# Attention scores as 64-row products in the two halves of TensorE's rows, in place of stacked 128-row products

## The chip, the cores and the metric

The kernel runs on one core of a Trainium2 chip. The metric is the device time of one execution in microseconds. Each run gives one time; the median of the runs is compared.

## The reference

One decoder block on x of 2048 positions and 1024 channels, with two branches that share a projection of the normalised input. The first branch is a gated linear recurrence (RG-LRU). The second is differential attention with 8 heads. Each head has two components of 64 channels, with softmax scores of their own, whose difference weighs v:

```python
u = rmsnorm(h, pre_g[l])
z = jnp.einsum('bsd,df->bsf', u, w_in[l])
xr, zr, q, k, v, za, gm = jnp.split(z, split_points, axis=-1)
...
s = jnp.einsum('bqhcd,bkhcd->bhcqk', q[:, q0:q1], k[:, :q1]).astype(jnp.float32) * scale
mask = (q0 + jnp.arange(Q_BLOCK))[:, None] >= jnp.arange(q1)[None, :]
s = jnp.where(mask, s, -jnp.inf)
p = jax.nn.softmax(s, axis=-1)
w = p[:, :, 0] - lam * p[:, :, 1]
outs.append(jnp.einsum('bhqk,bkhe->bqhe', w.astype(v.dtype), v[:, :q1]))
```

The attention's output is normalised and gated, both branches are projected, merged by sigmoid gates, projected once more, normalised and added to x. All inputs are float32.

## The kernel before

**Precision.** [...] To come near float32, an operand is split into a high and a low half of 16 bits (hi + lo), and a product a*b is made of hi*hi, hi*lo and lo*hi, added in PSUM. `mm3` (L187) does this for the projections: 8 blocks of 128 channels, 3 products each, 24 matmuls of 512 columns for one group.

**Stages.** First the recurrent branch (to about 488 us in the trace), then the attention (to about 1957 us), then the branches' projections and the output (to the end).

**The attention.** Its work is cut into units: one head h and one block t of 128 queries, so 8 x 16 units. Unit t has t + 1 blocks of 128 keys. `pieces` (L796) cuts these into one piece of up to 8 blocks (1024 columns) for t < 8, and two pieces from t = 8 on. A unit goes through these steps:

- `a_scores(u, ci)` (L800): the scores of component ci. For each piece it takes a PSUM tile `sc` of 128 x 1024 (the pool has two) and fills it in chunks of up to 512 columns, two matmuls a chunk (L814). VectorE then copies the piece to SBUF and takes its row maximum (L826), with the mask on the last block (L830).
- `a_exp` (L837): the bias from the maxima on VectorE (L845) and the exponentials on ScalarE (L851).
- `a_comb` (L854): VectorE combines the two components (L874), ScalarE rounds to the high half (L876), GpSimd makes the low half (L877), and two transposing DMAs on SP's queue bring both to `pt` (L880).
- `a_pv` (L886): the product with v, three matmuls of 128 columns for each block of keys (L897).

**How hi and lo are stacked.** A component has 64 channels, half of the array's 128 rows. K is kept as a tile of 128 rows for each component: its high half in rows 0 to 63, its low half in rows 64 to 127. Q is kept in two versions, (hi, lo) and (lo, hi). The matmul v = 0 gives hi*hi + lo*lo, the matmul v = 1 gives lo*hi + hi*lo, both over 128 rows. The projection, however, leaves both components side by side in the rows. So `split16` (L665) makes the halves in a tile `st` (ScalarE L667, VectorE L668), and `g_k` and `g_q` (L672, L685) copy pieces of `st` to their places by DMA on SP's queue: 4 transfers for a K tile, 6 for a Q tile. The copies are put into the list `later` and issued behind the next projection group.

**The order of work.** Between the attention's steps stand projection groups: k and q (`g_k`, `g_q`), v with its gate (`g_va`, 96 matmuls of 256 columns), and merge gates (`g_gm`). They are listed in `fills` (L743 to L763), together with entries that prepare weights and carry no group. Before a unit starts, all that it needs is made (`fill_to`, L946); beyond that, an accumulator lets in about (t + 10)/10 entries for each unit (L947, `per` is 28 for a head). The order within a unit is the string `ORD = "0fc1eFp"` (L35, L949): scores of component 0, one projection group if due, combination of the unit before, scores of component 1, exponentials, all other groups that are due, product with v of the unit two before (`LAG`). The framework's scheduler may still move instructions against each other where data allow.

Of the kernel before, what the change touches and what calls it, by code (L numbers as in the profile page):

```python
# [24 lines left out]
CH = 512  # L25
# [3 lines left out]
GM_T = 8   # groups of gate projections kept for the end of the attention  # L29
LAG = 2    # units between a unit's scores and its product with v  # L30
ACC0 = 8.0  # projection groups ahead of the attention units
PD = 5     # x tiles loaded ahead
# order in an attention unit: scores (0, 1), exponentials (e), combination of the unit before (c),
# product with v of an earlier one (p), with projection groups between them (f: one, F: all that are due)
ORD = "0fc1eFp"  # L35
SEG_A = 2  # where a head's gate projections stand between its chunks
# [7 lines left out]
def p2(e):  # L44
    return float(2.0 ** e)
# [3 lines left out]
def kernel(  # L49
# [44 lines left out]
    with ExitStack():  # L94
# [38 lines left out]
        def w16_at(i):  # L133
            """one of the four places for a block of weights"""
            return lambda w: w16_p.tile([128, 2, KD, 128], F16, tag=f"w{i % 4}", name="w16")
# [24 lines left out]
        def w_scale(w, ps, fac, keep=None):  # L160
            """power of two that brings the block's norm close to 2^13 (a rough sum is enough for it)"""
# [25 lines left out]
        def mm3(ps, w, c0, n):  # L187
            """ps[f128, n] += w^T u over all of d, s in [c0, c0 + n)"""
# [7 lines left out]
        # ================= RG-LRU branch =================  # L196
        with ExitStack() as lx:
# [21 lines left out]
            def prep_g(gr):  # L219
                """power of two that keeps the scaled, normalised input in fp16's range"""  # L220
# [58 lines left out]
            # weight pipeline  # L279
# [17 lines left out]
            def in_half(b, hf, z, w):  # L297
                """PSUM tile of a half row of an x_r (z = 0) or z_r (z = 1) block"""
# [144 lines left out]
            # per-channel vectors: rows of 128 channels, turned into columns  # L443
# [25 lines left out]
            with tc.issue_after(x_last[1]):  # L469
                # block-diagonal gate weights, exact f32r hi/lo  # L470
# [14 lines left out]
            with after_x():  # L485
                nc.vector.tensor_scalar(out=ba, in0=ba, scalar1=0.5, scalar2=None, op0=ALU.mult)
                nc.vector.tensor_scalar(out=bx, in0=bx, scalar1=0.5, scalar2=None, op0=ALU.mult)
                # softplus(-a) = max(-a, 0) + log1p(exp(-|a|)), log1p(t) = 2 atanh(t / (2 + t))
# [87 lines left out]
        # ================= differential attention and merge gates =================  # L576
# [3 lines left out]
        with ExitStack() as ax:  # L580
# [33 lines left out]
            def wadv(n):  # L614
                """weight blocks up to index n ready; two more on their way"""
# [49 lines left out]
            def split16(ps):  # L665
                st = sp.tile([128, 2, CH], F16, tag="st", name="st")
                nc.scalar.activation(st[:, 0], ps, AF.Copy, scale=p2(-14))  # L667
                nc.vector.scalar_tensor_tensor(out=st[:, 1], in0=ps, scalar=p2(-14), in1=st[:, 0],  # L668
                                               op0=ALU.mult, op1=ALU.subtract)
                return st  # L670

            def g_k(h, c):  # L672
                ps = ps_m.tile([128, CH], F32, tag="mm", name="mm")
                mm3(ps, wl["k", h], c * CH, CH)
                st = split16(ps)
                t = kp.tile([128, 2, CH], F16, tag="K", name="K")

                def mv():
                    for i in range(2):
                        nc.sync.dma_start(out=t[0:64, i, :], in_=st[64 * i:64 * i + 64, 0, :])  # L680
                        nc.sync.dma_start(out=t[64:128, i, :], in_=st[64 * i:64 * i + 64, 1, :])
                later.append(mv)
                Kt[h, c] = t

            def g_q(h, c):  # L685
                ps = ps_m.tile([128, CH], F32, tag="mm", name="mm")
                mm3(ps, wl["q", h], c * CH, CH)
                st = split16(ps)
                t = qp.tile([128, 2, 2, CH], F16, tag="Q", name="Q")

                def mv():
                    for i in range(2):
                        nc.sync.dma_start(out=t[0:64, :, i, :], in_=st[64 * i:64 * i + 64, :, :])
                        nc.sync.dma_start(out=t[64:128, 0, i, :], in_=st[64 * i:64 * i + 64, 1, :])
                        nc.sync.dma_start(out=t[64:128, 1, i, :], in_=st[64 * i:64 * i + 64, 0, :])
                later.append(mv)
                Qt[h, c] = t
# [102 lines left out]
            def a_scores(u, ci):  # L800
                h, t = u.h, u.t
                if ci == 0:
# [3 lines left out]
                col = 0  # L806
                for pi, (b0, nb) in enumerate(pieces(t)):
                    ps = ps_s.tile([128, 1024], F32, tag="sc", name="sc")
                    for x in range(0, nb, 4):
                        m = min(4, nb - x) * 128  # L810
                        K = Kt[h, (b0 + x) // 4]
                        q0 = (t % 4) * 128
                        for v in range(2):
                            nc.tensor.matmul(ps[:, x * 128:x * 128 + m], Qt[h, t // 4][:, v, ci, q0:q0 + 128],  # L814
                                             K[:, ci, 0:m], start=(v == 0), stop=(v == 1))
# [7 lines left out]
                    last = b0 + nb == t + 1  # L823
                    m = (nb - 1 if last else nb) * 128
# [384 lines left out]
```

## Time and profile before

| | |
|---|---|
| median of 3 runs | 2505.45 us (2501.87 to 2505.91) |
| span of the profiled execution, from its first to its last instruction | 2506.1 us |
| mean granted TensorE clock | 0.980 |
| DMA: packets, bytes | 541323, 268.73 MB |

No time other than the span is recorded for the profiled execution, so the span stands for it. It lies 0.65 us above the median of the runs.

In the profile, PE is TensorE's matmuls and PEld its weight loads, DVE is VectorE, ACT ScalarE, POOL GpSimd, and SP the queue that issues most DMAs. L814 is line 814 of the kernel. A row of a group has the line, the engine, the operation, output <- inputs, the shape and the count; behind the first bar the busy time in us and the mean of one in ns, and behind the second bar the engine's idle time just before, with what ended most of it. A row of waits reads: who waited, for whom, us in total, times, longest. A row of the timeline starts with the start and the length in us. A row of DMAs has the count, the size of one and the us from issue to landing. A row of a stretch has its length, then busy time and count of PE, PEld, DVE, ACT and POOL, the granted clock, the DMA share and GB/s.

### The profile page before, as it was taken

The page shows a single profiled execution, that of the slowest core. Times are in us where ns is not written, and L with a number is a line of the kernel's source. Part 1 is how long each engine was busy: PE and PEld are TensorE (multiplying, and loading weights), DVE is VectorE, ACT ScalarE, POOL GpSimd, SP SyncE. Part 2 cuts the span into 40 slices and gives each one's busy share as a digit, 9 for nine tenths or more (in the row PEclk, how much of TensorE's full clock was granted, in tenths as well). Part 3 has the DMA queues.
Part 4 walks back from the last instruction along what each step waited for, and adds up shares of the span by engine and source line. Part 5 has one row for each costly group of instructions (what it writes and reads, how often), then busy time and mean ns, then how long its engine had stood idle before and what let it go on. Part 6 is the DMA issues. An engine that isn't in the chain of part 4 may idle for free. (4 is left out here: it accounts for less than half of the span.)

```text
span 2506.1 us, 41430 instructions
## 1 busy us (share of the span) xinstructions
PE 2353.1 (94%) x15240; PEld 1355.3 (54%) x15240; DVE 1548.4 (62%) x4316; ACT 1224.6 (49%) x2156; POOL 679.7 (27%) x415
## 2 busy tenths in 40 slices
PE   6789999999998999998998999999999899999998
PEld 5344444465665665665665655655655444444443
DVE  8877667668658566667567478468467244633323
ACT  5555545456547546556456457356456244312211
POOL 3443334212222212222222222223123133322211
PEclk9899999999999999999999999999999999999999
DMA  9511111235444534635535445445445854743202
GB/s 244 104 43 48 46 42 34 76 81 119 108 96 111 113 84 108 127 82 113 115 84 114 103 96 118 95 90 124 95 90 115 251 177 135 239 148 118 84 17 101
DMA packets 541323, 268.73 MB, mean 107 GB/s; under 512 B 370504, under 2 KB 518016, under 8 KB 541120
## 3 DMA queue, kind: packets, MB, share of 16 engines
q1 hardware_dynamic: 538144, 256.74, 42.6%
q0 software_dynamic: 2816, 9.08, 1.2%
q8 instruction: 119, 1.95, 0.3%
q14 instruction: 84, 0.69, 0.1%
q10 hardware_dynamic: 160, 0.27, 0.0%
HBM read 110.79 MB, written 41.94 MB: 61 GB/s over the span
## 5 line engine op out<-in xcount | busy, mean ns | idle before, releaser
L192 PEld LDWEIGHTS <-w 128*128 128x128 f16 x5040 | 475.9, 100 | 576.5 <-issue 89.2
L192 PE MATMUL mm<-uT,w 128*128 128x512 f16 x3072 | 705.1, 383 | 12.9 <-ACT gm L728 8.9
L877 POOL TENSOR_TENSOR e<-e,e 128x1024 f16<-128x1024 f32 (+2 forms) x192 | 317.0, 1666 | 970.6 <-ACT e L876 487.0
L851 ACT ACTIVATE e<-e,nb,sc_h 128x1024 f32<-128x1024 f32 (+7 forms) x384 | 376.1, 980 | 160.8 <-DVE nb L845 125.6
L826 DVE TENSOR_SCALAR_CACHE_REDUCE e<-sc 128x1024 f32<-128x1024 f32 (+7 forms) x352 | 305.2, 880 | 134.9 <-PE sc L814 122.3
L192 PE MATMUL ps<-uT,w 128*128 128x512 f16 (+1 forms) x1968 | 354.4, 345 | 26.1 <-ACT xr L318 17.7
L711 PE MATMUL mm<-wva,uT 128*128 128x256 f16 x3072 | 352.7, 275 | 3.3 <-DVE st L668 2.6
L1094 PE MATMUL psb<-yt,w 128*128 128x512 f16 x1536 | 332.9, 379 | 2.0 <-ACT w L177 1.5
L711 PEld LDWEIGHTS <-uT 128*128 128x128 f16 x3072 | 301.5, 99 | 48.8 <-issue 2.9
L814 PE MATMUL sc<-K,Q 128*128 128x512 f16 (+3 forms) x1280 | 287.2, 351 | 19.9 <-DVE e L826 13.8
L897 PE MATMUL o<-V,pt 128*128 128x128 f16 x3264 | 224.5, 222 | 38.4 <-DMA pt<-e 38.1
L1094 PEld LDWEIGHTS <-w 128*128 128x128 f16 x1536 | 149.1, 98 | 184.9 <-issue 3.9
L897 PEld LDWEIGHTS <-pt 128*128 128x128 f16 x3264 | 200.0, 99 | 72.8 <-DMA pt<-e 46.5
L876 ACT ACTIVATE e<-e 128x1024 f16<-128x1024 f32 (+2 forms) x192 | 150.1, 802 | 143.1 <-DVE e L874 118.5
L814 PEld LDWEIGHTS <-Q 128*128 128x128 f16 x1280 | 119.6, 99 | 133.2 <-issue 20.2
L874 DVE SCALAR_TENSOR_TENSOR e<-e,rs,e 128x1024 f32<-128x1024 f32 (+2 forms) x192 | 190.0, 1017 | 2.2
L1125 PE MATMUL psf<-wo,m 128*128 128x512 f16 x720 | 155.7, 379 | 0.0
L156 ACT ACTIVATE jk<-wst 128x1024 bf16<-128x1024 f32 x80 | 84.2, 1052 | 138.7 <-DMA wst<-in_w_in_dram 102.6
L1125 PEld LDWEIGHTS <-m 128*128 128x128 f16 x768 | 75.1, 98 | 90.6
L1098 DVE SCALAR_TENSOR_TENSOR t<-gt,psb 128x512 f32<-128x512 f32 x64 | 43.8, 686 | 120.2 <-PE psb L1094 100.1
L1148 ACT ACTIVATE jk<-psf 128x1024 bf16<-128x1024 f32 x15 | 15.4, 1024 | 134.0 <-PE psf L1125 69.4
L717 DVE SCALAR_TENSOR_TENSOR V<-mm,V 128x256 f16<-128x256 f32 x64 | 26.9, 421 | 85.7 <-ACT V L716 85.6
(247 smaller groups left out, 2417.3 us busy)
## 6 DMA issues: line engine op xcount, KB each, us to landing
wst<-in_w_in_dram SPq DMA_DIRECT2D x64, 512.0 KB, 4.5
xt<-in_x_dram SPq DMA_DIRECT2D x32, 512.0 KB, 4.5
gm_d<-gm SPq DMA_DIRECT2D x64, 256.0 KB, 2.7
gt<-gm_d SPq DMA_DIRECT2D x32, 512.0 KB, 3.8
K<-st SPq DMA_DIRECT2D x128, 64.0 KB, 2.0
Q<-st SPq DMA_DIRECT2D x64, 128.0 KB, 2.4
Q<-st SPq DMA_DIRECT2D x128, 64.0 KB, 2.1
ya_d<-yT SPq DMA_DIRECT2D x64, 128.0 KB, 2.0
```

The costliest lines, as they stand in the source:

```text
L156: nc.scalar.activation(jk, w.st, AF.Square, accum_out=ss)
L192: nc.tensor.matmul(ps, w.t[:, a, k, :], uT[:, b, k, c0:c0 + n], start=(i == 0), stop=(i == 3 * KD - 1))
L711: nc.tensor.matmul(ps[:, j, :], uT[:, a, k, s0:s0 + 128], wt[:, b, k].rearrange("p t f -> p (t f)"), start=(i == 0), stop=(i == 3 * KD - 1))
L814: nc.tensor.matmul(ps[:, x * 128:x * 128 + m], Qt[h, t // 4][:, v, ci, q0:q0 + 128], K[:, ci, 0:m], start=(v == 0), stop=(v == 1))
L826: nc.vector.tensor_scalar(out=ev[:, 0:m], in0=ps[:, 0:m], scalar1=1.0, scalar2=None, op0=ALU.mult, op1=ALU.max, accum_out=u.mx[:, ci, col: ...
L851: nc.scalar.activation(ev[:, 0:nb * 128], ev[:, 0:nb * 128], AF.Exp, bias=nb_[:, ci:ci + 1], scale=sc_h[h], accum_out=u.sm[:, pi, ci:ci + 1])
L874: nc.vector.scalar_tensor_tensor(out=e0[:, 0:m], in0=e1v[:, 0:m], scalar=rs, in1=e0[:, 0:m], op0=ALU.mult, op1=ALU.add)
L876: nc.scalar.activation(e1[:, 0, 0:m], e0[:, 0:m], AF.Copy)
L877: nc.gpsimd.tensor_tensor(out=e1[:, 1, 0:m], in0=e0[:, 0:m], in1=e1[:, 0, 0:m], op=ALU.subtract)
L897: nc.tensor.matmul(o, pt[:, a, kb % 8, :], V[:, kb % 4, b, :], start=(kb == 0 and i == 0), stop=(kb == n - 1 and i == 2))
L1094: nc.tensor.matmul(ps, w.t[:, p, k, :], y_t[b][:, q, k, sl], start=(i == 0), stop=(i == 3 * KD - 1))
L1125: nc.tensor.matmul(pn[n], m16[:, a, j, ms], wo[:, b, j, ns], start=(j == 0 and a == 0 and b == 0), stop=(j == KD - 1 and a == 1))
```

## The change

K and Q stay as the projection leaves them: component 0 in rows 0 to 63, component 1 in rows 64 to 127, with hi and lo as two planes of one tile. `split16` writes straight into that tile; `st` and the copies go. The scores are three products of 64 rows each (hi*hi, hi*lo, lo*hi), and the two components alternate from matmul to matmul. `a_scores` now takes a piece instead of a component: step "0" of `ORD` makes piece 0 of both components, in both PSUM tiles, and step "1" makes piece 1 of both, or nothing for t < 8. VectorE's reads keep their shapes and number.

```diff
-            def split16(ps):
-                st = sp.tile([128, 2, CH], F16, tag="st", name="st")
-                nc.scalar.activation(st[:, 0], ps, AF.Copy, scale=p2(-14))
-                nc.vector.scalar_tensor_tensor(out=st[:, 1], in0=ps, scalar=p2(-14), in1=st[:, 0],
+            def split16(ps, t):
+                nc.scalar.activation(t[:, 0], ps, AF.Copy, scale=p2(-14))
+                nc.vector.scalar_tensor_tensor(out=t[:, 1], in0=ps, scalar=p2(-14), in1=t[:, 0],
                                                op0=ALU.mult, op1=ALU.subtract)
-                return st
...
-                st = split16(ps)
                 t = kp.tile([128, 2, CH], F16, tag="K", name="K")
-
-                def mv():
-                    for i in range(2):
-                        nc.sync.dma_start(out=t[0:64, i, :], in_=st[64 * i:64 * i + 64, 0, :])
-                        nc.sync.dma_start(out=t[64:128, i, :], in_=st[64 * i:64 * i + 64, 1, :])
-                later.append(mv)
+                split16(ps, t)
...
-                t = qp.tile([128, 2, 2, CH], F16, tag="Q", name="Q")
-
-                def mv():
-                    for i in range(2):
-                        nc.sync.dma_start(out=t[0:64, :, i, :], in_=st[64 * i:64 * i + 64, :, :])
-                        nc.sync.dma_start(out=t[64:128, 0, i, :], in_=st[64 * i:64 * i + 64, 1, :])
-                        nc.sync.dma_start(out=t[64:128, 1, i, :], in_=st[64 * i:64 * i + 64, 0, :])
-                later.append(mv)
+                t = qp.tile([128, 2, CH], F16, tag="Q", name="Q")
+                split16(ps, t)
...
-            def a_scores(u, ci):
+            def a_scores(u, pi):
...
-                col = 0
-                for pi, (b0, nb) in enumerate(pieces(t)):
-                    ps = ps_s.tile([128, 1024], F32, tag="sc", name="sc")
-                    for x in range(0, nb, 4):
-                        m = min(4, nb - x) * 128
-                        K = Kt[h, (b0 + x) // 4]
-                        q0 = (t % 4) * 128
-                        for v in range(2):
-                            nc.tensor.matmul(ps[:, x * 128:x * 128 + m], Qt[h, t // 4][:, v, ci, q0:q0 + 128],
-                                             K[:, ci, 0:m], start=(v == 0), stop=(v == 1))
+                if pi >= len(pieces(t)):
+                    return
+                b0, nb = pieces(t)[pi]
+                pss = [ps_s.tile([128, 1024], F32, tag="sc", name="sc") for _ in range(2)]
+                q0 = (t % 4) * 128
+                Q = Qt[h, t // 4]
+                for x in range(0, nb, 4):
+                    m = min(4, nb - x) * 128
+                    K = Kt[h, (b0 + x) // 4]
+                    for i, (a, b) in enumerate(((0, 0), (0, 1), (1, 0))):
+                        for ci in range(2):
+                            r = slice(64 * ci, 64 * ci + 64)
+                            nc.tensor.matmul(pss[ci][:, x * 128:x * 128 + m], Q[r, a, q0:q0 + 128], K[r, b, 0:m],
+                                             start=(i == 0), stop=(i == 2))
+                last = b0 + nb == t + 1
+                m = (nb - 1 if last else nb) * 128
+                for ci in range(2):
+                    ps = pss[ci]
```

The rest of `a_scores` stays, with the place of a maximum in `mx` counted from the piece's number.

More of the change, by code (lines that the diff above doesn't have):

```diff
@@ L687, in g_q @@
                 mm3(ps, wl["q", h], c * CH, CH)
-                st = split16(ps)
-                t = qp.tile([128, 2, 2, CH], F16, tag="Q", name="Q")
-                def mv():
-                    for i in range(2):
-                        nc.sync.dma_start(out=t[0:64, :, i, :], in_=st[64 * i:64 * i + 64, :, :])
-                        nc.sync.dma_start(out=t[64:128, 0, i, :], in_=st[64 * i:64 * i + 64, 1, :])
-                        nc.sync.dma_start(out=t[64:128, 1, i, :], in_=st[64 * i:64 * i + 64, 0, :])
-                later.append(mv)
+                t = qp.tile([128, 2, CH], F16, tag="Q", name="Q")
+                split16(ps, t)
                 Qt[h, c] = t
@@ L798, in pieces @@
                 return [(0, min(n, 8))] + ([(8, n - 8)] if n > 8 else [])
-            def a_scores(u, ci):
+            def a_scores(u, pi):
                 h, t = u.h, u.t
-                if ci == 0:
+                if pi == 0:
                     u.n = 1 if t == 0 else (2 if t <= 8 else 3)
@@ L822, in a_scores @@
                     u.e[ci, pi] = (e, ev)
-                    last = b0 + nb == t + 1
-                    m = (nb - 1 if last else nb) * 128
+                    col = pi
                     if m:
@@ L832, in a_scores @@
                                                        accum_out=u.mx[:, ci, col:col + 1])
-                        col += 1
             s0_t = {}
```

## The prediction

> **What bounds the kernel now.** I read the page's first lines, then the busy times by stretch, then the groups of TensorE by shape, the timeline of TensorE in the attention, and last the waits.
>
> ```profile
> span 2506.1 us, 41430 instructions
> PE 2353.1 (94%) x15240; PEld 1355.3 (54%) x15240; DVE 1548.4 (62%) x4316; ACT 1224.6 (49%) x2156; POOL 679.7 (27%) x415
> ```
>
> From the busy time of each engine in three stretches (PE, PEld, DVE, ACT and POOL in this order, then the granted clock):
>
> ```profile
> 500.00:700.00 200.00, 192.42 (x1473) 125.10 (x1471) 137.47 (x471) 115.19 (x240) 48.64 (x32) 0.99 0.46 103
> 1500.00:1700.00 200.00, 186.22 (x1387) 118.50 (x1385) 129.13 (x426) 107.28 (x220) 47.34 (x29) 0.97 0.47 103
> 1960.00:2506.00 546.00, 526.46 (x2442) 238.05 (x2440) 211.91 (x540) 135.90 (x195) 136.42 (x78) 0.99 0.44 141
> ```
>
> The attention, which the change touches, runs from about 488 to 1957 us. TensorE is busy there 186 to 192 us of every 200, VectorE 129 to 137, ScalarE 107 to 115. So TensorE sets the pace, with 8 to 14 us in 200 left, and time taken from it should mostly be seen in the span. VectorE comes second, at about two thirds.
>
> The matmuls of the scores (L814), of the product with v (L897) and of the weights' norm (L162), by shape:
>
> ```profile
> L814 PE MATMUL sc<-K,Q 128*128 128x512 f16 x896 | 237.4, 384 | 15.6 <-DVE e L826 13.8 <-DVE mx L830 1.6
> L897 PE MATMUL o<-V,pt 128*128 128x128 f16 x3264 | 224.5, 222 | 38.4 <-DMA pt<-e 38.1
> L814 PE MATMUL sc<-K,Q 128*128 128x384 f16 x128 | 31.5, 332 | 0.6 <-DVE mx L830 0.5
> L814 PE MATMUL sc<-K,Q 128*128 128x256 f16 x128 | 23.8, 272 | 0.2
> L814 PE MATMUL sc<-K,Q 128*128 128x128 f16 x128 | 17.5, 219 | 3.5 <-DMA Q<-st 3.0 <-issue 0.3 <-PE sc L814 0.2
> L162 PE MATMUL tot<-w_s,ones 128*128 128x1 bf16 x80 | 13.3, 167 | 28.4 <-DVE w_s L158 25.5 <-DVE w_sg_agm L107 1.5 <-DVE yme L111 1.1
> ```
>
> The mean duration of one (384 ns for 512 columns) isn't its cost, since matmuls overlap. The cost is the step from start to start, and the timeline gives it:
>
> ```profile
> 1191.59 1.03 PE L814 MATMUL sc<-K,Q 128*128 128x512 f16 x4
> 1192.45 0.39 PE L897 MATMUL o<-V,pt 128*128 128x128 f16 x4
> 1192.68 1.03 PE L814 MATMUL sc<-K,Q 128*128 128x512 f16 x4
> 1193.54 5.34 PE L192 MATMUL mm<-uT,w 128*128 128x512 f16 x24
> 1198.72 2.29 PE L897 MATMUL o<-V,pt 128*128 128x128 f16 x38
> 1200.84 10.66 PE L711 MATMUL mm<-wva,uT 128*128 128x256 f16 x96
> 1211.34 0.28 PE L814 MATMUL sc<-K,Q 128*128 128x128 f16 x2
> ...
> 1219.94 0.49 PE L814 MATMUL sc<-K,Q 128*128 128x384 f16 x2
> 1220.27 5.34 PE L192 MATMUL mm<-uT,w 128*128 128x512 f16 x24
> ```
>
> 24 matmuls of 512 columns go from 1193.54 to 1198.72, that is 216 ns each, and the four of the scores ahead of them take 0.86 us, 215 ns each. The 38 of 128 columns take 2.12 us, 56 ns each; the 96 of 256 columns 10.50 us, 109 ns each; the two of 384 columns 0.33 us, 165 ns each. Two things follow. Where one kind follows another (scores to product with v, scores to projection), no time is lost. And a slot of 56 ns holds a weight load too, for each matmul has its own: one load may come every 56 ns without being seen.
>
> **The change, part by part.**
>
> *The matmuls.* Before, a chunk of keys has 4 matmuls of 128 rows (2 components, 2 products). The 896 of 512 columns are 224 chunks, and each of the other widths has 32. At the steps above: 896 x 0.216 + 128 x (0.165 + 0.109 + 0.056) = 193.5 + 42.2 = 235.8 us. After, a chunk has 6 matmuls of 64 rows, in 3 pairs whose members read different halves of the rows and write different PSUM tiles. No row of this trace shows a pair, so its cost is bounded: below by one matmul of its width (216 ns), above by two (432 ns). I take the lower end, because a pair asks of the array what one row of L814 asks now: 128 rows of weights and one stream of 512 columns over all 128 rows. Its two weight loads need 112 ns at 56 each, which lies under 216 and 165, but is the limit for 256 and 128 columns. The sum is 672 x 0.216 + 96 x (0.165 + 0.112 + 0.112) = 145.2 + 37.3 = 182.5 us, 53.3 us less. At the upper end it is 1344 x 0.216 + 192 x 0.330 = 353.7 us, 117.9 us more.
>
> The Trainium skill speaks for the lower end: "TensorE: Matmul & The Clock Gate", Part 3, gives 3.07 times for four row tiles of 32 rows at 512 columns, and matmuls in different row groups start about 4 ns apart. No run shown here has this.
>
> *Going in and out of the halves.* Every other matmul of the attention uses all 128 rows, so each group of scores is now a change of the array's layout at its start and another at its end. There are 8 heads x (8 units with one piece + 8 with two) = 192 groups, 384 changes, if the scheduler neither joins nor splits them (the rows at 1191.59 to 1192.68 show one split). The trace has no such change. Its bounds: nothing, as between L814 and L897 now; or the whole passage of one column, 167 ns by the 1-column matmuls of L162, with a weight load of 99 ns behind it, since nothing could be loaded ahead:
>
> ```profile
> L814 PEld LDWEIGHTS <-Q 128*128 128x128 f16 x1280 | 119.6, 99 | 133.2 <-issue 20.2 <-DVE mx L830 4.0 <-DMA Q<-st 3.1
> ```
>
> That is 0 to 0.266 us each, 0 to 102 us in all. A gain is excluded, since nothing of today goes away with it. I take 56 ns, one load not hidden, since the trace hides loads in all other places and the columns of the next group can follow on. 384 x 0.056 = 21.5 us.
>
> The Trainium skill speaks against the change here: "TensorEngine Tiling (Array Packing)", Key Properties, says that a change of tiling mode drains TensorE. It states no time; what a drain would cost here is the second case below.
>
> *Both PSUM tiles at once.* There are two tiles for scores. Before, a group filled one, then the other, so VectorE emptied the first while the second was written. After, both fill together, are complete together (3 x 2 x 0.216 = 1.3 us), and the next group's first pair needs both. VectorE's reading of a full tile and the waits that end it:
>
> ```profile
> L826 DVE TENSOR_SCALAR_CACHE_REDUCE e<-sc 128x1024 f32<-128x1024 f32 x128 | 156.2, 1220 | 90.3 <-PE sc L814 80.5 <-PE tot L162 4.6 <-POOL e L877 4.1
> L826 DVE DVE_READ_ACCUMULATOR e<-sc 128x1 f32 x352 | 29.1, 83 | 0.0
> ```
>
> Two tiles take 2 x 1.30 = 2.6 us. Where a projection group (24 matmuls, 5.2 us) stands between the two groups of a unit, that is hidden. By stepping through the list of projection groups with its shares of (t + 10)/10 entries a unit, I find 18 of the 64 units with t >= 8 in which none is due between them. There TensorE would wait 2.6 us, where before it waited 0.4 (tile one is free at 4 x 0.216 + 1.30 = 2.16 us, TensorE is back at 8 x 0.216 = 1.73): up to 18 x 2.2 = 39 us. The cover is the product with v of an earlier unit, 27 to 48 matmuls of 56 ns (1.5 to 2.7 us), which the scheduler may put between, as it did at 1192.45. I take a quarter, 10 us.
>
> *No copies of K and Q.* The split now writes K and Q in place, and 320 transfers on SP's queue go, with their waits:
>
> ```profile
> K<-st SPq DMA_DIRECT2D x128, 64.0 KB, 2.0
> Q<-st SPq DMA_DIRECT2D x64, 128.0 KB, 2.4
> Q<-st SPq DMA_DIRECT2D x128, 64.0 KB, 2.1
> ...
> SPq L680 <- ACT st L667: 18.5, 8, 8.2
> ...
> SPq L695 <- ACT st L667: 13.4, 8, 2.7
> ```
>
> The transposes of the exponentials (L880) stand on the same queue, and TensorE waits 38.1 us in all for them (the L897 row above). The gain lies between 0 and 38 us, and a loss is excluded, as the queue gets nothing new. But SP's 32 us of waits for the split are small beside 186 us in which the transposes wait for their own data:
>
> ```profile
> SPq L880 <- ACT e L876: 185.9, 45, 13.8
> ```
>
> So I take 3 us. ScalarE and VectorE now write into the buffers that the scores read, and might have to wait for a free one. They don't: the matmuls of a projection stand behind the last scores that read the old Q (by the order of the list, in all 30 cases), and TensorE works in order. The reads by VectorE, the exponentials, the combination and the product with v keep their count and shapes: nothing.
>
> *Sum.* -53.3 + 21.5 + 10 - 3 = -24.8 us. Against the profiled execution's span of 2506.1 us that is 2481.3. The median of the runs shown, 2505.45, lies 0.65 us below that span, so I forecast 2481 us.
>
> **The rivals.**
>
> *The array drains at each change.* If the array must be empty before its layout changes, one passage of 167 ns is paid each time: 384 x 0.167 = 64.1 us, more than the matmuls save. -53.3 + 64.1 + 10 - 3 = +17.8, 2523 us; with the load of 99 ns behind each drain +55.8, 2561 us. It decides from (53.3 - 7)/384 = 121 ns a change. For it: changes are many, and a group's work is short (0.3 to 1.3 us). Against it: nothing in the trace shows TensorE waiting for its own pipeline between kinds. The Trainium skill's page "TensorEngine Tiling (Array Packing)", Key Properties, has this as a rule.
>
> *The pairs run one after the other.* Then the halves of the rows bring nothing, and the change doesn't do what it says: 1920 matmuls instead of 1280 at the same steps, +117.9 - 3 = +115, 2620 us. For it: in this trace every 512-column matmul starts 216 ns after the last, whatever it reads. Against it: no pair of that trace could have run together, as each used all rows.
>
> *VectorE takes the gain.* The 18 units wait their whole 39 us: -53.3 + 21.5 + 39 - 3 = +4, 2510 us, and if the changes cost somewhat less, no difference. For it: where no projection is due, four full tiles cost VectorE 5.2 us a unit and the combination two times 1.3 more, while TensorE has about as little. Against it: VectorE idles 80.5 us waiting for scores.
>
> **How the numbers follow.** The forecast's case has 0.48, the drain 0.27, one after the other 0.13, VectorE 0.12. A difference under 0.2% (5 us) can't be told from none by a measurement of this kernel. The forecast is faster but for 0.02; the drain is slower in 0.24, and 0.02 and 0.01 of it fall to the same and to faster, where its price is near 121 ns; VectorE's case splits into 0.03 faster, 0.08 same, 0.01 slower; one after the other is slower. Faster 0.50, same 0.12, slower 0.38. The range starts at 2448, where the changes cost nothing and the queue gives a little more (2506.1 - 53.3 - 5), and ends at 2563, the drain with its load. It leaves out the pairs one after the other and a few hundredths at each end. The likeliest case alone spans 2448 to 2501.
>
> **What would show it.** In the changed profile's timeline, a group of six 512-column scores should take about 0.65 us from the first start to the next kind's start, if pairs run together; 1.3 us says one after the other. The gap from the last score to the next 128-row matmul, beyond 216 ns, and the gap ahead of the first score, give the price of a change: 0 to 0.06 us right, 0.12 and more wrong. TensorE's waits for VectorE's L826 should grow from 13.8 to about 24 us, those for the transposes shrink a little, and the lines K<-st and Q<-st be gone. The prediction is wrong if score groups take twice their time, or if TensorE's idle time between groups grows by more than 46 us.

## The result, and the profile after

The change makes the kernel slower: 2573.07 us, the median of 4 runs (2572.5 to 2582.22), against 2505.68 us before (4 runs). The ratio is 1.0275, with a 95% interval of 1.0256 to 1.0295. The forecast was 2481 us, in a range from 2448 to 2563. The profiled execution is the slowest of the four (span 2580.4 us), so about 9 us of what it shows is not in the median.

The page's first lines of the changed kernel, and TensorE in two of the stretches shown before (columns as there):

```profile
span 2580.4 us, 42036 instructions
PE 2437.9 (94%) x15880; PEld 1336.8 (52%) x15880; DVE 1542.7 (60%) x4316; ACT 1226.6 (48%) x2156; POOL 664.2 (26%) x415
```

```profile
500.00:700.00 200.00, 192.85 (x1462) 114.00 (x1460) 133.36 (x465) 114.45 (x236) 44.81 (x31) 0.97 0.40 86
1500.00:1700.00 200.00, 192.39 (x1457) 112.61 (x1456) 125.81 (x423) 108.47 (x220) 46.33 (x29) 0.98 0.39 85
```

TensorE is at least as busy in these stretches as before, and the attention lasts longer (to about 2038 us, before to 1957): TensorE has more to do, not less. The scores by shape (L804 is the old L814, L889 the old L897):

```profile
L804 PE MATMUL sc<-K,Q 64*128 64x512 f16 x1344 | 254.3, 388 | 25.6 <-DVE e L819 15.2 <-DVE mx L823 10.0
L889 PE MATMUL o<-V,pt 128*128 128x128 f16 x3264 | 223.6, 221 | 16.3 <-DMA pt<-e 16.1
L804 PE MATMUL sc<-K,Q 64*128 64x384 f16 x192 | 30.7, 325 | 3.4 <-DVE e L819 2.6 <-DVE mx L823 0.8
L804 PE MATMUL sc<-K,Q 64*128 64x256 f16 x192 | 25.0, 278 | 1.9 <-DVE mx L823 1.9
L804 PE MATMUL sc<-K,Q 64*128 64x128 f16 x192 | 15.0, 218 | 0.7 <-ACT Q L666 0.7
```

Rows of different shapes overlap in time, so their busy times don't add up. Taken together, the scores keep TensorE busy for 311.8 us, against 287.2 before. Had every pair run as one, that would have fallen. The timeline of TensorE in the changed kernel says why, in one stretch:

```profile
1180.44 1.47 PE L804 MATMUL sc<-K,Q 64*128 64x512 f16 x6
1181.83 5.41 PE L696 MATMUL mm<-wva,uT 128*128 128x256 f16 x48
...
1193.96 1.22 PE L889 MATMUL o<-V,pt 128*128 128x128 f16 x19
1195.12 1.47 PE L804 MATMUL sc<-K,Q 64*128 64x512 f16 x12
1196.52 0.18 PE L162 MATMUL tot<-w_s,ones 128*128 128x1 bf16 x1
```

Read the distance from a row's start to the next row's start. Twelve products of 512 columns take 1196.52 - 1195.12 = 1.40 us; six others take 1.39 us. The twelve are six pairs, at 216 ns a pair. The six must be the products of one component alone, at 216 ns each, since the members of a pair mostly start 3 ns apart. So the chip does run pairs as one, but the scheduler often took the components apart: over the whole trace, 545 of the 960 possible pairs start within 40 ns of each other; 79 groups of six and 58 groups of three hold no pair.

The same rows show another loss. Six steps of 216 ns are 1.30 us, and 1.39 passed: 93 ns are lost behind the scores. Ahead of them, 19 products with v at 56 ns are 1.06 us, and 1.16 passed: 96 ns are lost there. Before, neither end lost anything. The median over the 266 groups is the same: 96 ns in, 93 ns out. The weight loads show it as time in which they waited for nothing visible ("issue"), first of the change, then of before:

```profile
L804 PEld LDWEIGHTS <-Q 64*128 64x128 f16 x1920 | 112.2, 95 | 193.3 <-issue 80.4 <-DVE mx L823 13.4 <-DVE s L859 1.7
PEld L192 <- issue: 126.8, 277, 8.4
```

```profile
PEld L192 <- issue: 89.2, 160, 6.6
```

The waits of TensorE in the changed kernel moved little in sum. For the transposes they fell from 38.1 us, for VectorE's reads they rose (13.8 us on L826 and 2.1 on L830 before):

```profile
PE sc L804 <- DVE e L819: 17.8, 11, 4.7
PE o L889 <- DMA pt<-e: 16.1, 14, 2.6
PE sc L804 <- DVE mx L823: 12.7, 10, 3.8
```

A third loss stands in the trace's record of the granted clock: at times TensorE runs at half of it. One such stretch of the changed kernel (columns as in the stretches above), and two rows of its timeline:

```profile
1408.00:1418.00 10.00, 9.67 (x35) 3.92 (x36) 7.48 (x37) 7.46 (x12) 0.00 (x0) 0.50 0.57 126
```

```profile
1408.33 2.74 PE L804 MATMUL sc<-K,Q 64*128 64x512 f16 x6 [0.63 <-DVE mx L823]
1411.00 0.61 PE L889 MATMUL o<-V,pt 128*128 128x128 f16 x4
```

The granted clock is 0.50, and six products that took 1.39 us above take 1411.00 - 1408.33 = 2.67 us. Over the trace, products of 512 columns start 427 ns apart in such stretches, and 216 ns elsewhere. From the first score to the last product with v, TensorE has half its clock for 89 us, before for 48. What its steps take longer for it, waits left out, is 43 us, before 21. So 22 of the 74 us between the two spans are a lower clock, a term that the prediction doesn't have. The profiled execution has the lowest granted clock of the four, 0.973. By the 0.975 of a middle one it is (1 - 0.975) x 2571 us against (1 - 0.980) x 2504 before, about 14 us; this is an estimate, and rather high, because half a clock costs nothing while TensorE waits.

In the traces of before, of the change and of e7_three (below), 37 of 38 such stretches in the attention begin right behind 3.4 us in which TensorE sat idle for 1.6 us or more; at a random place it sits idle for 0.1 to 0.2 of 3.4 us on average. So a wait can cost more than itself. Many waits are followed by no such stretch, and why the change, with no more waits in all, has more of them isn't known.

### The profile page after: what moved, and what is told of

It is laid out like the page before. It is cut to its first block, busy times and chain, and to the rows that moved or that the text cites. A ratio compares the mean times of both kernels' runs of the same rounds, so it can differ in the third digit from the quotient of the medians.

```text
span 2580.4 us, 42036 instructions
## 1 busy us (share of the span) xinstructions
PE 2437.9 (94%) x15880; PEld 1336.8 (52%) x15880; DVE 1542.7 (60%) x4316; ACT 1226.6 (48%) x2156; POOL 664.2 (26%) x415
## 5 line engine op out<-in xcount | busy, mean ns | idle before, releaser
L192 PEld LDWEIGHTS <-w 128*128 128x128 f16 x5040 | 469.4, 100 | 601.9 <-issue 126.8
L192 PE MATMUL mm<-uT,w 128*128 128x512 f16 x3072 | 715.4, 387 | 10.6 <-ACT gm L713 6.3
L869 POOL TENSOR_TENSOR e<-e,e 128x1024 f16<-128x1024 f32 (+2 forms) x192 | 307.9, 1617 | 1064.8 <-ACT e L868 600.3
L804 PE MATMUL sc<-K,Q 64*128 64x512 f16 (+3 forms) x1920 | 311.8, 354 | 31.6 <-DVE e L819 17.8
L1086 PEld LDWEIGHTS <-w 128*128 128x128 f16 x1536 | 149.4, 98 | 185.2 <-issue 4.8
L889 PE MATMUL o<-V,pt 128*128 128x128 f16 x3264 | 223.6, 221 | 16.3 <-DMA pt<-e 16.1
L889 PEld LDWEIGHTS <-pt 128*128 128x128 f16 x3264 | 193.1, 99 | 65.2 <-issue 24.7
L804 PEld LDWEIGHTS <-Q 64*128 64x128 f16 x1920 | 112.2, 95 | 193.3 <-issue 80.4
L866 DVE SCALAR_TENSOR_TENSOR e<-e,rs,e 128x1024 f32<-128x1024 f32 (+2 forms) x192 | 184.7, 989 | 2.4
L823 DVE CUSTOM_DVE_ANT_0 e<-sc,mask 128x128 f32<-128x128 f32 x256 | 72.6, 286 | 32.7 <-PE sc L804 31.5
L854 DVE TENSOR_TENSOR s<-sm 128x2 f32<-128x2 f32 x64 | 10.2, 159 | 135.6 <-ACT e L843 135.4
```

The costliest lines, as they stand in the source:

```text
L192: nc.tensor.matmul(ps, w.t[:, a, k, :], uT[:, b, k, c0:c0 + n], start=(i == 0), stop=(i == 3 * KD - 1))
L804: nc.tensor.matmul(pss[ci][:, x * 128:x * 128 + m], Q[r, a, q0:q0 + 128], K[r, b, 0:m], start=(i == 0), stop=(i == 2))
L866: nc.vector.scalar_tensor_tensor(out=e0[:, 0:m], in0=e1v[:, 0:m], scalar=rs, in1=e0[:, 0:m], op0=ALU.mult, op1=ALU.add)
L869: nc.gpsimd.tensor_tensor(out=e1[:, 1, 0:m], in0=e0[:, 0:m], in1=e1[:, 0, 0:m], op=ALU.subtract)
L889: nc.tensor.matmul(o, pt[:, a, kb % 8, :], V[:, kb % 4, b, :], start=(kb == 0 and i == 0), stop=(kb == n - 1 and i == 2))
L1086: nc.tensor.matmul(ps, w.t[:, p, k, :], y_t[b][:, q, k, sl], start=(i == 0), stop=(i == 3 * KD - 1))
```

## The experiments

Theory A: the loss is products that run alone, since the scheduler takes the components apart, and some 0.19 us for each visit to the half-row layout. The rivals are named in the expectations. All runs were made beside the kernel before on the same chip. Where the text gives us above or below before, they are worked out from the ratio, and can differ by up to 3 us from the difference of the two medians.

| run | what it is | median us | before us | ratio (95%) |
|---|---|---|---|---|
| e1_onetile | pairs kept together | 2547.52 | 2500.44 | 1.0185 (1.0168 to 1.0202) |
| e2_serial | one component after the other | 2581.39 | 2500.44 | 1.0313 (1.0296 to 1.033) |
| e3_serial128 | the same, 128 rows | 2601.58 | 2500.44 | 1.0399 (1.0384 to 1.0415) |
| e4_three128 | TensorE's work of ideal pairs | 2482.18 | 2500.44 | 0.9927 (0.9912 to 0.9942) |
| e5_nocopy | before without copies | 2489.67 | 2501.92 | 0.9947 (0.9928 to 0.9966) |
| e6_piecewise | before in the order by pieces | 2519.31 | 2501.92 | 1.006 (1.0037 to 1.0082) |
| e7_three | before with three products of four | 2503.11 | 2501.92 | 1.0002 (0.9991 to 1.0013) |
| e8_half | pairs, tiles of 512 columns | 2550.27 | 2501.92 | 1.0186 (1.0165 to 1.0208) |
| e9_onetile128 | onetile with three 128-row products | 2490.84 | 2502.33 | 0.9954 (0.9938 to 0.9969) |
| e10_lag3 | onetile, one unit further behind | 2531.08 | 2502.33 | 1.012 (1.0092 to 1.0147) |
| e11_scalar | before, copies on ScalarE's queue | 2507.04 | 2502.33 | 1.002 (1.0009 to 1.0032) |
| e11_gpsimd | before, copies on GpSimd's queue | 2517.4 | 2502.33 | 1.0057 (1.0038 to 1.0076) |
| e12_visit64 | before with 384 visits | 2541.64 | 2503.39 | 1.0151 (1.0136 to 1.0166) |
| e13_visit128 | its control | 2506.55 | 2503.39 | 1.0016 (1.0007 to 1.0026) |
| e14_lag3_128 | onetile128, one unit further behind | 2477.93 | 2503.39 | 0.9903 (0.9882 to 0.9925) |
| e15_lag3_before | before, one unit further behind | 2507.81 | 2503.67 | 1.0017 (1.0005 to 1.0029) |

**Are the pairs broken up, and by what?** *e1_onetile*:

```diff
-                pss = [ps_s.tile([128, 1024], F32, tag="sc", name="sc") for _ in range(2)]
+                sc = ps_s.tile([128, 2, 1024], F32, tag="sc", name="sc")
+                pss = [sc[:, 0], sc[:, 1]]
```

with `ps_s` at one buffer.

> The changed kernel, but both components of a piece share one PSUM tile of two halves (pool of one), so that neither can be started without the other; the order of issue then has the two components alternating everywhere, and 196 groups of scores instead of 266. Theory A (the loss is products that run alone because the scheduler took the components apart, 415 of 960 pairs, plus about 0.19 us for each visit to the half-row layout): the scores' steps fall from 253 to about 183 us and 70 visits fall away (13 us), so 2573 - 83 = 2490 us, up to 2528 if TensorE then waits for both halves to be read. Rival B (pairing matters little, the loss is TensorE waiting for VectorE to empty both tiles): no better than the change, 2560 us or more.

Measured: 46 us above before, where the change is 69 above: 23 us better, and not the 45 to 83 of theory A. The busy time of the scores did fall as forecast, and the timeline has pairs everywhere (957 of 960):

```profile
L805 PE MATMUL sc<-K,Q 64*128 64x512 f16 x1344 | 177.1, 390 | 30.2 <-DVE e L820 20.1 <-DVE s L860 4.2 <-DVE mx L824 3.8
L805 PE MATMUL sc<-K,Q 64*128 64x384 f16 x192 | 22.9, 339 | 4.5 <-DVE mx L824 2.6 <-DVE w_iv_agm L115 1.8 <-DVE e L820 0.2
L805 PE MATMUL sc<-K,Q 64*128 64x256 f16 x192 | 15.9, 271 | 2.0 <-DVE e L820 2.0
L805 PE MATMUL sc<-K,Q 64*128 64x128 f16 x192 | 11.2, 222 | 0.7 <-ACT Q L666 0.7
```

```profile
728.74 1.47 PE L805 MATMUL sc<-K,Q 64*128 64x512 f16 x12
730.14 5.42 PE L696 MATMUL mm<-wva,uT 128*128 128x256 f16 x48
```

Taken together, the scores keep TensorE busy for 219.1 us, 93 less than in the change, from one edit in how PSUM is taken. So it was the two separate tiles that let the scheduler start one component without the other. But only 23 of these 93 us reached the end; rival B, with 2560 us or more, is missed too. The waits of TensorE in onetile show where a part went:

```profile
PE o L890 <- DMA pt<-e: 63.8, 43, 5.4
PE sc L805 <- DVE e L820: 22.3, 17, 3.6
```

TensorE waits 64 us for the transposes, in the change 16. The step of theory A that a saved microsecond of TensorE is a saved microsecond at the end doesn't hold.

*e8_half* has one PSUM tile for 512 columns of both components, and two of it:

```diff
+                    sc = ps_s.tile([128, 2, CH], F32, tag="sc", name="sc")
```

> Pairs as in onetile, but the PSUM tile holds 512 columns of both components and there are two of it, so that VectorE reads the first while the second is written; VectorE reads in pieces of up to 512 columns, so in more instructions. 244 groups of scores. Theory A with F: steps 57 us less than before, 244 x 0.19 = 46 us for the visits, few waits for VectorE: within 10 us of before, well ahead of onetile (2547). Rival: VectorE's extra instructions cost what the second tile saves, 2540 us or more.

Measured: 46 us above before, no better than onetile, so theory A with F missed. The rival's 2540 us or more is what came; whether VectorE's extra instructions are the reason (1553 us of work, 1544 in onetile) wasn't tried apart. TensorE waits 33.5 us for the transposes (63.8 in onetile), but 40.4 for VectorE's reads:

```profile
PE sc L813 <- DVE e L822: 40.4, 17, 6.2
PE o L893 <- DMA pt<-e: 33.5, 27, 4.8
```

One wait took the place of the other.

*e2_serial* keeps an order by hand (the framework's `issue_after`), the three products of one component, then the three of the other:

```diff
-                    for i, (a, b) in enumerate(((0, 0), (0, 1), (1, 0))):
-                        for ci in range(2):
+                    for i, (a, b), ci in [(i, p, ci) for ci in (1, 0) for i, p in enumerate(((0, 0), (0, 1), (1, 0)))]:
...
```

> The changed kernel with the three 64-row products of one component in a row, then the three of the other, so that no two neighbours use different halves; order kept by hand. 299 groups. Theory A (a pair takes the time of one): every product is paid alone, 354 us of steps instead of 253, and 33 more visits at 0.19 us: 2573 + 107 = 2680 us. Rival C (pairs bring nothing, start times 3 ns apart are only how the profiler writes them down): within 10 us of the change, 2565 to 2585 us.

Measured: 78 us above before, 9 more than the change and far from 107 more. The order didn't do what I meant: the last product of one component and the first of the next lie in different halves too, and they overlap; 572 pairs start within 40 ns, a few more than in the change. So this run can't tell A from C. Its neighbour does:

*e3_serial128* has the same order with `r = slice(0, 128)`.

> The same order of issue as the run with the products in a row, but each product uses all 128 rows, so that it sums over both components and the scores are not those of the reference; the layout of the array never changes. Theory A (0.19 us for each visit): 299 x 0.19 = 57 us less than the run with 64 rows, about 2623 us. Rival D (the layout change is free, the gaps at the groups' ends come from waits that stay): the same time as the run with 64 rows, 2680 us or so, within 10.

Measured: 100 us above before, 20 more than with 64 rows, where theory A expected 57 less. With 128 rows nothing overlaps, as twelve products show:

```profile
743.11 2.75 PE L805 MATMUL sc<-K,Q 128*128 128x512 f16 x12
745.70 4.53 PE L696 MATMUL mm<-wva,uT 128*128 128x256 f16 x40
```

2.59 us, and nothing lost at the end, beside 1.40 us for twelve in the halves. The steps of all scores are 353 us against 243 in e2_serial. Thus the halves won 110 us of steps there by chance neighbours and lost 299 visits, 57 us at 0.19. The pair really takes the time of one, and rival C falls; rival D falls too, since the gaps at the groups' ends are gone with 128 rows. Of the 53 us that are left 20 reached the end; e2_serial's trace loses 30 us by half clock, that of e3_serial128 12.

**What does a visit cost?** *e9_onetile128* is onetile with these three products in place of the six:

```diff
+                    for ci, a, b, s, e in ((0, 0, 0, True, False), (1, 1, 0, True, True), (0, 0, 1, False, True)):
+                        nc.tensor.matmul(pss[ci][:, x * 128:x * 128 + m], Q[:, a, q0:q0 + 128], K[:, b, 0:m],
+                                         start=s, stop=e)
```

> The run onetile (both components in one PSUM tile) with three products of 128 rows a chunk in place of three pairs of 64: two for component 0, one for component 1, so the scores are not those of the reference. The same steps of TensorE, about as many groups (190), no change of layout. Theory A (0.19 us for each visit to the half rows, paid in the span): 196 x 0.187 = 37 us less than onetile, about 2510 us. Rival H (in the span the visits are hidden, as TensorE waits for others anyway: the run three, with 59 us less work, was no faster): 2535 to 2550 us.

Measured: 11.5 us faster than before, so 1.0185 - 0.9954 = 2.3%, or 58 us, lie between it and onetile. They have the same steps, tiles and almost the same groups (190 and 196), and differ in the layout. The direction is theory A's, the size is more: 0.29 us a visit, where the gaps at the two ends add up to 0.187. Rival H falls.

*e12_visit64* and *e13_visit128* put visits into the kernel before, with all else as it was (`0:64`, in the control `0:128`):

```diff
+                        if x == 0:
+                            nc.tensor.matmul(ps[:, 0:1], Qt[h, t // 4][0:64, 0, ci, q0:q0 + 128], K[0:64, ci, 0:1],
+                                             start=True, stop=True)
```

> The kernel before with one more matmul ahead of each piece of scores: 64 rows, one column, into a column that the piece's first product then writes anew. 384 visits to the half-row layout and nothing else. Theory A (0.187 us at the two ends of a visit, paid in the span) with one slot of 0.03 to 0.06 us: 72 us more than visit128. Theory A2 (a visit also makes later waits longer, 0.29 us as between onetile and onetile128): 110 us more than visit128. Rival H (visits vanish in waits): less than 35 us more than visit128.

> The same with 128 rows in the added matmul: 384 slots of 0.03 to 0.06 us without a change of layout. All theories: 0 to 25 us slower than before, 2502 to 2527.

Measured: 38 and 3 us above before, so 1.35%, or 34 us, between them for 384 visits: 0.09 us each, just inside rival H and half of theory A. At TensorE the price is there. In visit64 the timeline reads

```profile
1180.32 0.17 PE L814 MATMUL sc<-K,Q 64*128 64x1 f16 x1
1180.43 1.04 PE L817 MATMUL sc<-K,Q 128*128 128x512 f16 x4
1181.40 0.17 PE L814 MATMUL sc<-K,Q 64*128 64x1 f16 x1
1181.50 0.93 PE L817 MATMUL sc<-K,Q 128*128 128x512 f16 x4
```

Four products of 512 columns are 0.86 us, and 0.97 pass before the next visit; the one-column product, a slot of 28 ns in the control, takes 0.11. The medians are 96 ns in and 78 out, 384 x 0.174 = 67 us. Shorter waits paid about half of it back: in the attention TensorE is idle for 36 us in visit64 and 66 in visit128. Most of that are the waits for the transposes, visit64 first, then visit128:

```profile
PE o L900 <- DMA pt<-e: 14.2, 16, 2.7
```

```profile
PE o L900 <- DMA pt<-e: 36.0, 29, 2.7
```

TensorE came later to the product with v, and so waited 22 us less for it. A visit costs 0.17 to 0.19 us of TensorE; what reaches the end depends on what TensorE would have waited for: 0.09 us here, 0.29 between onetile128 and onetile. Onetile's trace has, beside the gaps, 19 us more idle time in the attention than that of onetile128 and 6 us more lost by half clock; why the visits should bring these isn't settled.

**Where does TensorE's saved time go?** *e4_three128* is the change with three products of 128 rows for a chunk, as in onetile128, in the two separate tiles and in an order kept by hand.

> The changed kernel with three products of 128 rows for a chunk in place of six of 64: one for component 1 and two for component 0, so the scores are not those of the reference. TensorE has the work of ideal pairs without a change of layout. Theory A: 53 us less than the kernel before, 2453 us, up to 2475 if VectorE or the transposes take part of it. Rival E (TensorE's time in the scores is not what sets the end): within 10 us of the kernel before, 2495 to 2515 us.

Measured: 18 us faster than before (14 to 22). The steps of the scores fell by 59 us in its trace. Less than a third reached the end: between theory A and rival E. The missing copies and the order by pieces, tried apart below, are part of these 18. *e7_three* does the same to the kernel before in its own order:

```diff
-                        for v in range(2):
+                        for v in range(2 - ci):
...
-                                             K[:, ci, 0:m], start=(v == 0), stop=(v == 1))
+                                             K[:, ci, 0:m], start=(v == 0), stop=(v == 1 - ci))
```

> The kernel before in its own order, component by component, with three products of 128 rows a chunk and not four: the second product of component 1 is left out, so its scores are not those of the reference. TensorE has 59 us less in the scores. Theory F (the order by pieces is what ate the gain of three128): 45 to 59 us faster than before, 2441 to 2455. Rival G (a faster TensorE only waits for VectorE and the transposes): about 18 us faster, as three128.

Measured: no difference (0.9991 to 1.0013). Fifty-nine microseconds of TensorE's work are gone, and nothing is gained. This is the plainest finding of the study. Rival G had 18 us here; even that was too much. TensorE's busy time and its waits in e7_three:

```profile
PE 2305.4 (92%) x14920; PEld 1327.2 (53%) x14920; DVE 1551.7 (62%) x4316; ACT 1223.5 (49%) x2156; POOL 672.9 (27%) x415
```

```profile
PE o L897 <- DMA pt<-e: 57.8, 43, 4.8
PE tot L162 <- DVE w_s L158: 37.0, 15, 10.5
...
PE sc L814 <- DVE e L826: 20.8, 14, 3.5
```

Busy time fell from 2353 to 2305 us. Its waits rose by 20 us for the transposes, 12 for the weights' norm (25.5 before), 7 for VectorE's reads. That busy time fell by 48 us, for 59 us less work, is mostly the clock: with more waits there is more half clock. The granted clock of its ten runs is 0.969 to 0.976, that of the runs before beside them 0.978 to 0.982. In the attention of each trace (from the first score to the last product with v), in us:

| trace | length | TensorE idle | at half clock | lost by half clock |
|---|---|---|---|---|
| before | 1469 | 68 | 48 | 21 |
| change | 1558 | 62 | 89 | 43 |
| e1_onetile | 1524 | 119 | 74 | 33 |
| e5_nocopy | 1461 | 62 | 21 | 9 |
| e7_three | 1460 | 108 | 79 | 28 |
| e9_onetile128 | 1461 | 100 | 61 | 27 |

In e7_three 40 us of the 59 went into waits and 7 into the lower clock, and its attention is 9 us shorter than before; in the medians of the runs nothing of that is left. VectorE's work is the same and its share hardly rose (62%): no engine is full. What probably holds is the way of each unit from scores to the transposed exponentials, through VectorE, ScalarE, GpSimd and SP's queue in order; the waits point there, but no run shows it by itself.

*e6_piecewise* takes the change's order alone, on stacked rows (`a_scores(u, pi)` with the two products of before).

> The kernel before with its stacked 128-row products and copies, only that a step makes one piece of both components, in both PSUM tiles, as in the change, and no longer both pieces of one component. Theory F (filling both tiles at once makes TensorE wait for VectorE): 15 to 37 us slower than before, 2515 to 2537. Rival G (the order does no harm; three128 gained 18 us and not 59 because VectorE and the transposes can't follow a faster TensorE): within 5 us of before.

Measured: 15 us slower (9 to 21). The order by pieces, in both tiles at once, costs that: near the lower end of theory F, whose forecast for e7_three failed.

*e10_lag3*, *e14_lag3_128* and *e15_lag3_before* move the product with v one unit further behind (`LAG = 3`; `tp` at 6 buffers in the first two, 4 in the last).

> The run onetile with the product with v three units behind the scores, not two, and six tiles for the transposed exponentials, not four. In onetile TensorE waited 64 us for the transposes, before 38. Theory J (the time that pairs save is given back in waits for the transposes): 20 to 45 us faster than onetile, 2500 to 2527. Rival K (it is given back in waits for VectorE to read the PSUM tile): within 8 us of onetile, 2540 to 2555.

> The run onetile128 (TensorE's work of ideal pairs, no change of layout, scores not those of the reference) with the product with v three units behind and six tiles for the transposed exponentials. Theory J (part of what TensorE saves goes into waits for the transposes): 10 to 30 us faster than onetile128, 2461 to 2481. Rival K (it goes into waits for VectorE): within 8 us of it, 2483 to 2499.

> The kernel before with the product with v three units behind the scores, the four tiles for transposed exponentials as they are (six don't fit). Theory J (TensorE's waits for the transposes, 38 us, shrink where a unit needs one such tile): 5 to 15 us faster than before, 2488 to 2498. Rival: with four tiles the transposes of units of two pieces wait for room, and the distance brings nothing or costs: 2500 to 2515.

Measured: 16 us better than onetile (1.012 against 1.0185), 13 better than onetile128 (0.9903 against 0.9954), and 4 worse than before, in the last: theory J missed there, and the rival's 2500 to 2515 us came. That the four tiles leave no room is its reason, and wasn't tried apart. In e10_lag3 the wait for the transposes fell from 63.8 to 27.5 us, that for VectorE's reads rose from 22.3 to 32.5:

```profile
PE sc L805 <- DVE e L820: 32.5, 17, 10.0
PE o L890 <- DMA pt<-e: 27.5, 19, 3.1
```

Theory J holds in direction; in e10_lag3 it is short of its lower end (20), in e14_lag3_128 within its range. Even so the pairs, with the visits, are 30 us slower than before.

**What were the copies worth?** *e5_nocopy* keeps before's order and two products, on K and Q as the split leaves them.

> The kernel before, but K and Q stay as the split leaves them and the 320 copies go; the two 128-row products a chunk stay, on unstacked halves, so the scores are not those of the reference. It shows what the copies alone are worth. Theory A of the prediction: about 3 us, so 0 to 8 us faster than before. Rival: the queue's relief reaches the transposes that TensorE waits for, 20 to 38 us faster.

Measured: 13 us faster (9 to 18), between the two. *e11_scalar* and *e11_gpsimd* keep the copies and change the queue (`nc.scalar.dma_start`, `nc.gpsimd.dma_start`).

> The kernel before with the copies of K and Q issued on ScalarE's queue, not SP's. Leaving the copies out gained 12 us. Theory L (it was the place on SP's queue, ahead of the transposes): 5 to 12 us faster than before. Rival M (it was the transfers or the time until K and Q are in place): within 4 us of before, or slower if ScalarE, at 49% busy, loses time on the issues.

> The same on GpSimd's queue, which is 27% busy. Theory L: 5 to 12 us faster than before. Rival M: within 4 us, or slower if GpSimd's low halves of the exponentials come later for it.

Measured: 5 us and 14 us slower. Theory L's forecast is missed twice, which speaks against the place on SP's queue as the cost. It isn't ruled out, for these runs can't part what SP's queue gains from what ScalarE or GpSimd loses with the issues. Whether it is the transfers or the time until K and Q are in place wasn't tried. Part of the 13 us may be the clock: in its trace e5_nocopy loses 9 us by half clock in the attention, before 21.

## Why the prediction was wrong, point by point

**"Its cost is bounded ... I take the lower end."** A pair does take the time of one, as forecast: 1.40 us for twelve. The step that failed is the count behind it, "672 x 0.216": it took for granted that all pairs are issued as pairs. 415 of 960 were not, because each component has a PSUM tile of its own (with one tile for both, 957 ran as pairs); that the scheduler starts whichever is free fits this, but wasn't looked at. The sum of the steps became 253 us and not 182.5: 70 us on this term. No rival had it; the rival "one after the other" stands for a chip that can't run pairs, and its 2620 us lies near e3_serial128's 2602, where nothing overlaps. A smaller slip went the other way: the 112 ns for narrow pairs were too many. In onetile a pair of 256 columns takes 109 ns and one of 128 columns 56, two weight loads and all, and its steps add up to 179 us.

The Trainium skill, "TensorE: Matmul & The Clock Gate", Part 3, has matmuls of different row groups start about 4 ns apart. The trace agrees where they are neighbours: 3 or 4 ns in 327 of the 545 pairs, 10 to 14 in most others.

**"I take 56 ns, one load not hidden."** Measured 96 ns on the way in and 93 out (78 behind a single column), inside the bounds of 0 to 266 and below the 121 from which the drain was to decide. The number of changes was too small as well: 266 groups, 532 changes, and not 384. At about 94 ns they make 50 us in place of 21.5: 28 us on this term. They lie between the prediction's own two signs, 0 to 0.06 us for right and 0.12 and more for wrong. The drain, as a rival, was right in that each change costs more than a hidden load; its price of 167 ns was not.

The Trainium skill, "TensorEngine Tiling (Array Packing)", Key Properties, states that a change of tiling mode drains TensorE. The gaps agree in that each change costs, and only where the rows change: 96 and 93 ns here, none in e3_serial128. Whether TensorE drains meanwhile can't be read from them.

**"Both PSUM tiles at once": 10 us.** e6_piecewise measures 15 (9 to 21). Right in size for this order by itself; in the change's own trace TensorE's idle time in the attention didn't rise, but fell by 6 us.

**"No copies": 3 us.** e5_nocopy measures 13. The argument looked at SP's queue alone, and the two runs with other queues don't bear it out.

**"TensorE sets the pace ... time taken from it should mostly be seen in the span."** This failed, and it would have made a good share of the forecast wrong even with perfect pairs: e7_three takes 59 us off and gains nothing. e9_onetile128 and e4_three128 have the steps of perfect pairs, no copies and no change of layout, for which the prediction's terms give -53.3 + 10 - 3 = -46 us; they gain 11.5 and 18. TensorE was busy 190 of 200 us, but it wasn't the bound alone: what it saved was spent in waits for the transposes and VectorE, and in the lower clock that came with them. A row against the forecast stood in the prediction itself: 38.1 us of waits for the transposes, which I only used for the copies.

**The sum.** Terms measured one by one seem to close: +17.6 us of steps (253 against 235), 50 for the changes, 15 for the order and -13 for the copies are +70, beside +69 measured in the medians. That is luck, since the last two were measured in other kernels. In the change's own trace the attention is 89 us longer: 18 of steps, 50 for the changes, 22 for the lower clock, 7 of projection work that before lay ahead of it, and 6 less of waits, as near as steps can be told apart. The stages around it are 15 us shorter. The prediction had no term for the clock and took waits for fixed; but work added to TensorE reaches the end by half (visit64) to nearly whole (e3_serial128), work taken away hardly at all. One slip of arithmetic changes nothing: the range's upper end, 2563, stands for the drain with its load, for which the sum gives 2561.

## What to carry to other kernels

An alternation that the chip needs must be forced by what the scheduler sees, here by one PSUM tile for both partners; two tiles leave it free to break them up. Count the changes of TensorE's row layout, not the columns saved: at some 0.19 us a visit, a group must save about one product of 512 columns (0.216 us) only to break even. Before costing an engine's saving as a gain, look at what it waits for already, and take out the work in a trial (as e7_three does): a busy share of 95% is not yet a bound. And compare the granted clock of two traces before a difference is put down to work or waits.

## What the runs showed of the hardware that was not expected

Products in different halves overlap wherever they are neighbours, also across the border of two chains: e2_serial, meant to have no pairs, had 572. And the change of layout costs at both ends about alike, 96 ns in and 78 to 93 out, though a weight load alone is hidden in slots of 56 ns elsewhere in these traces. Stretches of half clock, in which 512 columns take 427 ns and not 216, nearly always begin right behind waits of TensorE, and cost 21 us in the attention of before and 43 in that of the change.
